# A hybrid encoder layer on one core: the attention mask added by VectorE, one copy of the attention's products out of PSUM, paced weight splits, and queries loaded a head ahead

## The chip, the core and the metric

The kernel runs on one core of one Trainium2 chip. The metric is the device time of one execution in microseconds, taken as the median of several runs. The engines are named as the profile names them: PE is TensorE (its weight loads are PEld), DVE is VectorE, ACT is ScalarE, POOL is GpSimd, and SP is SyncE, whose queue issues nearly all DMAs.

## What is computed

One layer of a post-norm encoder on 1024 prompt frames and 32 frames of a running stream (1056 together), width 1024, 8 heads of 64, in float32:

```python
p = x @ w_in      # GLU pair | q | k | v | forget logits | two branch gates
u = a * sigmoid(b); y_conv = (silu(LN(depthwise_conv31(u) + b_dw))) @ w_conv_out
c = cumsum(log_sigmoid(p_f + b_f))                     # per head
s = (q @ k.T) / 8 + c_q - c_k
s = where(k_pos <= q_pos, s, -1e30)                    # causal mask
o = softmax(s) @ v
m = sigmoid(g_conv) * y_conv + sigmoid(g_attn) * (o @ w_attn_out)
x1 = LN1(alpha * x + m @ w_o)
y = LN2(alpha * x1 + square(relu(x1 @ w_up)) @ w_down)
```

The streams attend to 512 cached keys and values besides their own 32. Keys, values, log forget values and the last 30 convolution rows are outputs too.

## The kernel before, in words

Everything is held transposed, features on partitions. A float32 operand is split into two fp32r parts, `hi` (ACT, a rounding copy) and `lo` (DVE or POOL, the rest), and a product is three matmuls: hi by hi, hi by lo, lo by hi. `Weights` (`W`) loads the tiles of the big matrices by halves into `raw` (four halves held), splits them (`split`, lines 336 to 350) and holds up to `RB` = 4 split tiles; `W.engine` says which engine makes `lo` (POOL in the attention stage). `W.ahead` is called at every `I.service()`; `W.take` splits on demand what is not split yet.

The order of instructions on PE, ACT, DVE and POOL is that of the program; DMAs on SP's queue are ordered by the framework. A planner (`Issue`, `I`) keeps an estimated clock for each engine while the program is written. `I.fill(*need)` puts steps of other work, the *filler*, into PE's order as long as the needed tiles are not due by these clocks and a quota is left. In the attention stage the filler is the branch gates' product (`gates`, tiles 6 to 15, six matmuls of 352 columns a step) and then the first two tiles of the convolution branch's projection (`early`, `ps_yc`).

The attention stage (lines 842 to 1173) works through units: eight prompt heads of eight row blocks (`Rows`, block `r` has 128 queries and `n` = 128 (r + 1) keys), and behind heads 2 to 5 one `Stream` each, two heads of the running stream against the cache. Row blocks are pipelined: one turn of the loop at line 1152 issues the scores of block `a0`, then the reciprocal of `a1`, the product with the values of `a3` (every second block, two blocks at a time, 256 queries), the transposes of `a2`, the exponential of `a0`, the normalization of `a1` and the `lo` subtractions of `a2`.

- `scores` (line 1025): two matmuls for each 512 keys into `ps_s`, of which two buffers exist, then the mask as a product of a bf16 identity and a bf16 mask tile with 1e30 above the diagonal, added into the last 128 columns (the scores are negated). `softmax_a` takes the row minimum on DVE.
- `weigh` is the exponential on ACT with its sum, `norm` the division by it on DVE, `turn` the transposes through `ps_tr` and the split into `th` (ACT) and `tl` (DVE).
- `fold` (line 994): the product with the values, `ps_pv`, has the part with `v`'s hi on partitions 0 to 63 and that with its lo on 64 to 127. ACT copies both halves out into two tiles `oa` and `ob`, POOL adds them and splits the sum into `oh` and `ol`. `ps_pv` takes its buffer from the two of `ps_tr`.
- `load_head` (line 863) issues a head's nine loads: keys `k1` and `k2`, queries `q1` and `q2`, values `v`. `load(n + 1)` calls it at the third row block of the unit before, or, behind a `Stream`, when that starts.

Of the kernel before, what the change touches and what calls it, by code (L numbers as in the profile page):

```python
# [9 lines left out]
F32 = mybir.dt.float32  # L10
F32R = mybir.dt.float32r
# [6 lines left out]
P = 128  # L18
D = 1024
SEQ = 1024  # L20
# [9 lines left out]
H = 8  # L30
# [15 lines left out]
RB = 4  # L46
# [221 lines left out]
def hybrid_layer(ctx: ExitStack, tc, io):  # L268
# [54 lines left out]
    class Weights:  # L323
        def __init__(self):
            self.raw, self.parts, self.taken, self.done, self.halves = [], [], 0, 0, 0
            self.engine, self.limit = "dve", NWO + 1

        def load(self, queue=None):
            i = len(self.raw)
# [22 lines left out]
        def ahead(self):  # L352
            while len(self.raw) < 2 * self.limit and held["raw"] < RAWB:
                self.load()
            while self.halves < len(self.raw) and I.ready(self.raw[self.halves]) <= I.t["pe"] and \
                    (self.halves % 2 or self.halves // 2 in kept or held["parts"] < RB):
                self.split()
                if len(self.raw) < 2 * self.limit:
                    self.load()

        def take(self):
            self.ahead()
# [479 lines left out]
    with pool("b") as pb, pool("pb", space=PSUM) as psb:  # L842
# [17 lines left out]

        def load_head(h, i):
            hr = slice(h * DH, (h + 1) * DH)
            k1 = pb.tile([P, 2 * NKS], F32R, tag=f"k1{i % 2}", bufs=1, name=f"k1_{h}")
            q1 = pb.tile([P, SEQ], F32R, tag=f"q1{h % 2}", bufs=1, name=f"q1_{h}")
            k2, q2 = k2s[i % 2], q2s[h % 2]
            v = pb.tile([P, 10, P], F32R, tag=f"v{i % 2}", bufs=1, name=f"v_{h}")
            queue = nc.gpsimd if h == 0 else None
            dma(k1[0:DH, 0:SEQ], qk_s["kh"][hr, 0:SEQ], queue)  # L870
            dma(k1[DH:P, 0:SEQ], qk_s["kh"][hr, 0:SEQ], queue)
            dma(q1[0:DH], qk_s["qh"][hr, 0:SEQ], queue)
            dma(q1[DH:P], qk_s["ql"][hr, 0:SEQ], queue)
            dma(k2[0:DH, 0:SEQ], qk_s["kl"][hr, 0:SEQ], queue)
            dma(k2[DH:DH + 2, 0:SEQ].rearrange("s (t i) -> s t i", i=P), crows[0][h, :, 0:NT, :], queue)
            dma(q2[0:DH], qk_s["qh"][hr, 0:SEQ], queue)
            dma(q2[DH + 2:DH + 4, :].rearrange("s (t i) -> s t i", i=P), crows[1][h, :, 0:NT, :], queue)
            dma(v[:, 0:NT, :], v_s[h])
            return k1, k2, q1, q2, v

# [113 lines left out]
        def fold(pv, n, tag, outs, parts=1, into=None):  # L994

            at = 0 if into is None else into[0]
            pr = slice(at, at + DH)
            a, b = (pb.tile([P, 256], F32, tag=x, bufs=1, name=f"{x}_{tag}")[pr, :parts * n] for x in ("oa", "ob"))
            act(a, pv[0:DH, :parts * n], AF.Copy)
            act(b, pv[DH:P, :parts * n], AF.Copy)  # L1000
            tt(a, a, b, ADD, "pool")
            if parts > 1:
                tt(a[:, :n], a[:, :n], a[:, n:], ADD, "pool")
                a = a[:, :n]
            if into is None:
                oh, ol = (pb.tile([DH, 256], F32R, tag=x, bufs=2, name=f"{x}_{tag}")[:, :n] for x in ("oh", "ol"))
            else:
                oh, ol = (t[pr, into[1]] for t in last_o)
            I.run("pool", n * 3.0 + 120, [oh], [a])
            nc.gpsimd.tensor_copy(oh, a)  # L1010
            tt(ol, a, f32(oh), SUB, "pool")
            for cols, dst in outs:
                for i, t in enumerate((oh, ol)):
                    if dst[0].start < 6 * DH:
                        dma(o_s[i][dst], t[:, cols])
                    else:
                        dma(last_o[i][dst[0].start - 6 * DH:dst[0].stop - 6 * DH, dst[1]], t[:, cols])

        class Rows:
# [5 lines left out]
            def scores(self):  # L1025
# [5 lines left out]
                for a in range(0, n, 512):  # L1031
                    w = min(512, n - a)
                    mm(ps[:, a:a + w], q1[:, qc], k1[:, a:a + w], True, False)
                    mm(ps[:, a:a + w], q2[:, qc], k2[:, a:a + w], False, a + w < n)
                mm(ps[:, n - P:n], ident_b, mask_b, False, True)
                self.sm = softmax_a(ps[:, :n], n, tag)

            def weigh(self):
# [42 lines left out]
        class Stream:  # L1081


            def __init__(self, ops, g):
                self.ops, self.g = ops, g

            def scores(self):
                k1, k2, q1, q2, _ = self.ops
# [46 lines left out]
        def work():  # L1135
            for n, (kind, h) in enumerate(units):
# [5 lines left out]
                for i, r in enumerate(ROWS):  # L1142
                    if i % 2 == 0:
                        pair = []
                    if i == 2:
                        load(n + 1)
                    yield Rows(ops, h, r, pair)

        act(tiny, eps, AF.Exp)
        a1 = a2 = a3 = None  # L1150
        I.quota = Q0
        for a0 in chain(work(), (None,) * 3):
            I.quota += ((16 - GA + YM / 2) * 12 - Q0) / (H * NT + H // 2)
            if a0:
# [6 lines left out]
                a2.turn()  # L1161
            if a0:
                a0.weigh()
            if a1:
                a1.norm()
            if a2:
# [2 lines left out]
            I.service()  # L1169
            a1, a2, a3 = a0, a1, a2  # L1170
        act(tiny, eps, AF.Sigmoid)
        while I.step(True):
            pass

# [805 lines left out]
```

## Time and profile before

| | |
|---|---|
| median of 3 runs | 1444.24 us (1443.33 to 1444.28) |
| profiled execution | 1444.01 us, its span 1441.4 us |
| PE busy | 1425.4 us, 99% of the span |
| DVE, ACT, POOL busy | 1119.5, 683.0, 124.2 us |
| granted clock of PE | 0.998 of full speed (2.4 GHz) |
| attention stage | some 329 to 575 us of the span |

The span runs from the first to the last instruction of the profiled execution; its time has some 2.6 us more around it. An engine's busy time is the union of its instructions. Matmuls are pipelined, so one matmul's listed duration is longer than the distance to the next one's start.

### The profile page before, as it was taken

To read this page: it belongs to the slowest core of one execution; us is meant where nothing else is said; L and a number is where in the kernel's file an instruction comes from. 1 tells how busy PE (TensorE), PEld (TensorE's weight loads), DVE (VectorE), ACT (ScalarE), POOL (GpSimd) and SP (SyncE) were. 2 spreads that over 40 slices of the span, in tenths; PEclk is the share of its full clock that TensorE was granted. 3 is DMA by queue.
4 is the path that set the end of the run, shared out by engine and by line. 5 is a ranking of instruction groups with operands and counts; after the bars stand their busy time and mean duration, and the time that the engine had idled before them with its cause. 6 is when DMAs were issued, how large, how long until landed. Compare 5 with 4: busy or idle time off the path is not lost.

```text
span 1441.4 us, 27988 instructions
## 1 busy us (share of the span) xinstructions
PE 1425.4 (99%) x10623; PEld 1404.0 (97%) x10623; DVE 1119.5 (78%) x1929; ACT 683.0 (47%) x1446; POOL 124.2 (9%) x183
## 2 busy tenths in 40 slices
PE   9999999999999999999999999999999999999996
PEld 8999999999999999999999999999999999999996
DVE  6998899865666655855797888888976789889668
ACT  5123433465665656543345666676657323321134
POOL 0000000023455533000000000000000000000000
PEclk9999999999999999999999999999999999999999
DMA  7125554287455557425343348766689999884212
GB/s 249 46 61 161 171 172 157 88 273 209 111 152 157 154 153 264 144 83 177 94 135 124 130 151 296 251 239 231 225 287 344 335 317 333 276 321 176 67 45 77
DMA packets 157441, 267.91 MB, mean 186 GB/s; under 512 B 22680, under 2 KB 81272, under 8 KB 157308
## 3 DMA queue, kind: packets, MB, share of 16 engines
q1 hardware_dynamic: 156348, 263.98, 55.4%
q0 software_dynamic: 544, 1.59, 0.5%
q8 instruction: 84, 1.38, 0.4%
q10 hardware_dynamic: 416, 0.56, 0.1%
q14 instruction: 49, 0.40, 0.1%
HBM read 168.29 MB, written 97.74 MB: 185 GB/s over the span
## 4 chain that ended last, share of the span: by engine, by line
PE 97%; DVE 1%; DMA 1%; ACT 0%; issue 0%; SPq 0%; DVEq 0%
PE ps_u L206 18%; PE ps_d L206 17%; PE ps_g L206 13%; PE ps_dn L206 6%; PE ps_o L206 6%; PE ps_up L206 5%; PE ps_v L206 3%; PE ps_yc L206 3%; PE ps_k L206 3%; PE ps_glua L206 3%; PE ps_q L206 3%; PE ps_glub L206 3%; PE ps_yo L206 3%; PE ps_s L206 3%; PE ps_pv L206 2%; PE ps_tr L210 2%
## 5 line engine op out<-in xcount | busy, mean ns | idle before, releaser
L235 DVE SCALAR_TENSOR_TENSOR ca<-u,prm,ca 128x1086 f32<-128x1086 f32 x120 | 161.7, 1347 | 2.4
L206 PE MATMUL ps_g<-xh,whi 128*128 128x352 f32 x384 | 131.7, 343 | 0.0
L218 ACT ACTIVATE swhi<-s 128x512 fp32r<-128x512 f32 x100 | 61.9, 624 | 146.9 <-DVE s L227 134.0
L206 PE MATMUL ps_g<-xh,wlo 128*128 128x352 f32 x384 | 123.7, 322 | 0.0
L206 PE MATMUL ps_g<-xl,whi 128*128 128x352 f32 x384 | 121.5, 322 | 0.0
L206 PE MATMUL ps_u<-tl,swhi 128*128 128x264 f32 x416 | 118.4, 285 | 0.0
L206 PE MATMUL ps_u<-th,swhi 128*128 128x264 f32 x416 | 118.2, 284 | 0.0
L206 PE MATMUL ps_u<-th,swlo 128*128 128x264 f32 x416 | 118.2, 284 | 0.0
L218 ACT ACTIVATE whi<-raw 128x512 fp32r<-128x512 f32 (+1 forms) x120 | 69.6, 624 | 69.6 <-PE ps_glua L206 29.7
L227 DVE TENSOR_TENSOR tl<-ps_tr,th 128x512 fp32r<-128x512 f32 (+2 forms) x96 | 51.4, 552 | 60.2 <-ACT th L218 59.5
L206 PE MATMUL ps_d<-hu_h,swhi 128*128 128x264 f32 x480 | 93.0, 285 | 0.1
L206 PE MATMUL ps_d<-hu_l,swhi 128*128 128x264 f32 x480 | 92.9, 285 | 0.0
L218 ACT ACTIVATE r<-r 128x528 f32<-128x528 f32 (+1 forms) x120 | 73.9, 616 | 37.8 <-DVE r L227 35.5
L227 DVE TENSOR_TENSOR wlo<-raw,whi 128x512 fp32r<-128x512 f32 (+1 forms) x100 | 64.8, 686 | 29.1 <-ACT whi L218 28.9
L227 DVE TENSOR_TENSOR r<-r,ps_u 128x528 f32<-128x528 f32 x91 | 62.6, 699 | 29.6 <-PE ps_u L206 29.6
L206 PEld LDWEIGHTS ps_u<-th,swhi 128*128 128x128 f32 x416 | 78.3, 188 | 0.0
L206 PEld LDWEIGHTS ps_u<-th,swlo 128*128 128x128 f32 x416 | 78.3, 188 | 0.0
L206 PEld LDWEIGHTS ps_u<-tl,swhi 128*128 128x128 f32 x416 | 78.2, 188 | 0.0
L227 POOL TENSOR_TENSOR acc<-acc,lnrest 128x288 f32<-128x288 f32 x4 | 3.0, 787 | 857.6 <-ACT lnrest L218 857.6
L206 PEld LDWEIGHTS ps_d<-hu_h,swhi 128*128 128x128 f32 x480 | 74.6, 189 | 0.3 <-issue 0.2
L206 PEld LDWEIGHTS ps_d<-hu_l,swhi 128*128 128x128 f32 x480 | 74.6, 189 | 0.0
L206 PEld LDWEIGHTS ps_g<-xh,whi 128*128 128x128 f32 x384 | 72.7, 189 | 0.7
(434 smaller groups left out, 4997.8 us busy)
## 6 DMA issues: line engine op xcount, KB each, us to landing
h_s<-sp SPq DMA_DIRECT2D x84, 528.0 KB
raw<-in_w_in_dram SPq DMA_DIRECT2D x63, 256.0 KB
hu_h<-h_s SPq DMA_DIRECT2D x30, 528.0 KB
hu_l<-h_s SPq DMA_DIRECT2D x30, 528.0 KB
sraw<-in_w_up_dram SPq DMA_DIRECT2D x52, 256.0 KB
hu<-h_s SPq DMA_DIRECT2D x24, 528.0 KB
sraw<-in_w_ds_dram SPq DMA_DIRECT2D x48, 256.0 KB
g_s<-gt SPq DMA_DIRECT2D x48, 176.0 KB
```

What stands on the lines that cost most here:

```text
L206: self.nc.tensor.matmul(ps, lhsT=w, rhs=x, start=start, stop=stop)
L210: self.nc.tensor.transpose(ps, x, ident)
L218: self.nc.scalar.activation(out, in_, func, **kw)
L227: (self.nc.vector if eng == "dve" else self.nc.gpsimd).tensor_tensor(out, a, b, op)
L235: self.nc.vector.scalar_tensor_tensor(out, a, s, b, op0, op1)
```

## The change

The mask product of a row block becomes an addition by DVE on the last 128 columns of `ps_s` (the streams keep theirs). `fold` copies all 128 partitions of `ps_pv` to `ob` in one ACT instruction; POOL copies the half that lies on the other partitions to `oa`, and adds. In the attention stage (`paced`) `W.ahead` no longer splits; one half is split behind the exponential of a row block of more than 256 columns, and on demand. The four query loads leave `load_head` and are issued at the third row block of the head before, ahead of the next unit's loads.

```diff
--- before.py
+++ after.py
@@ -323,7 +323,7 @@
     class Weights:
         def __init__(self):
             self.raw, self.parts, self.taken, self.done, self.halves = [], [], 0, 0, 0
-            self.engine, self.limit = "dve", NWO + 1
+            self.engine, self.limit, self.paced = "dve", NWO + 1, False
 
         def load(self, queue=None):
             i = len(self.raw)
@@ -352,11 +352,18 @@
         def ahead(self):
             while len(self.raw) < 2 * self.limit and held["raw"] < RAWB:
                 self.load()
-            while self.halves < len(self.raw) and I.ready(self.raw[self.halves]) <= I.t["pe"] and \
-                    (self.halves % 2 or self.halves // 2 in kept or held["parts"] < RB):
+            while not self.paced and self.step():
+                pass
+        def step(self):
+            i = self.halves
+            if i < len(self.raw) and I.ready(self.raw[i]) <= I.t["pe"] and (i % 2 or i // 2 in kept or held["parts"] < RB):
                 self.split()
                 if len(self.raw) < 2 * self.limit:
                     self.load()
+                return True
+            return False
 
         def take(self):
             self.ahead()
@@ -860,21 +867,31 @@
 
 
 
+        queries = {}
+        def load_queries(h, queue=None):
+            hr = slice(h * DH, (h + 1) * DH)
+            q1 = pb.tile([P, SEQ], F32R, tag=f"q1{h % 2}", bufs=1, name=f"q1_{h}")
+            q2 = q2s[h % 2]
+            dma(q1[0:DH], qk_s["qh"][hr, 0:SEQ], queue)
+            dma(q1[DH:P], qk_s["ql"][hr, 0:SEQ], queue)
+            dma(q2[0:DH], qk_s["qh"][hr, 0:SEQ], queue)
+            dma(q2[DH + 2:DH + 4, :].rearrange("s (t i) -> s t i", i=P), crows[1][h, :, 0:NT, :], queue)
+            queries[h] = q1, q2
         def load_head(h, i):
             hr = slice(h * DH, (h + 1) * DH)
             k1 = pb.tile([P, 2 * NKS], F32R, tag=f"k1{i % 2}", bufs=1, name=f"k1_{h}")
-            q1 = pb.tile([P, SEQ], F32R, tag=f"q1{h % 2}", bufs=1, name=f"q1_{h}")
-            k2, q2 = k2s[i % 2], q2s[h % 2]
+            k2 = k2s[i % 2]
             v = pb.tile([P, 10, P], F32R, tag=f"v{i % 2}", bufs=1, name=f"v_{h}")
             queue = nc.gpsimd if h == 0 else None
             dma(k1[0:DH, 0:SEQ], qk_s["kh"][hr, 0:SEQ], queue)
             dma(k1[DH:P, 0:SEQ], qk_s["kh"][hr, 0:SEQ], queue)
-            dma(q1[0:DH], qk_s["qh"][hr, 0:SEQ], queue)
-            dma(q1[DH:P], qk_s["ql"][hr, 0:SEQ], queue)
+            if h == 0:
+                load_queries(h, queue)
+            q1, q2 = queries[h]
             dma(k2[0:DH, 0:SEQ], qk_s["kl"][hr, 0:SEQ], queue)
             dma(k2[DH:DH + 2, 0:SEQ].rearrange("s (t i) -> s t i", i=P), crows[0][h, :, 0:NT, :], queue)
-            dma(q2[0:DH], qk_s["qh"][hr, 0:SEQ], queue)
-            dma(q2[DH + 2:DH + 4, :].rearrange("s (t i) -> s t i", i=P), crows[1][h, :, 0:NT, :], queue)
             dma(v[:, 0:NT, :], v_s[h])
             return k1, k2, q1, q2, v
 
@@ -995,10 +1012,12 @@
 
             at = 0 if into is None else into[0]
             pr = slice(at, at + DH)
-            a, b = (pb.tile([P, 256], F32, tag=x, bufs=1, name=f"{x}_{tag}")[pr, :parts * n] for x in ("oa", "ob"))
-            act(a, pv[0:DH, :parts * n], AF.Copy)
-            act(b, pv[DH:P, :parts * n], AF.Copy)
-            tt(a, a, b, ADD, "pool")
+            a, b = (pb.tile([P, 256], F32, tag=x, bufs=1, name=f"{x}_{tag}")[:, :parts * n] for x in ("oa", "ob"))
+            act(b, pv[:, :parts * n], AF.Copy)
+            a = a[pr]
+            I.run("pool", parts * n * 1.0 + 120, [a], [b])
+            nc.gpsimd.tensor_copy(a, b[DH - at:P - at])
+            tt(a, a, b[pr], ADD, "pool")
             if parts > 1:
                 tt(a[:, :n], a[:, :n], a[:, n:], ADD, "pool")
                 a = a[:, :n]
@@ -1031,8 +1050,8 @@
                 for a in range(0, n, 512):
                     w = min(512, n - a)
                     mm(ps[:, a:a + w], q1[:, qc], k1[:, a:a + w], True, False)
-                    mm(ps[:, a:a + w], q2[:, qc], k2[:, a:a + w], False, a + w < n)
-                mm(ps[:, n - P:n], ident_b, mask_b, False, True)
+                    mm(ps[:, a:a + w], q2[:, qc], k2[:, a:a + w], False, True)
+                tt(ps[:, n - P:n], ps[:, n - P:n], mask_b, ADD)
                 self.sm = softmax_a(ps[:, :n], n, tag)
 
             def weigh(self):
@@ -1082,7 +1101,7 @@
 
 
             def __init__(self, ops, g):
-                self.ops, self.g = ops, g
+                self.ops, self.g, self.n = ops, g, NKS
 
             def scores(self):
                 k1, k2, q1, q2, _ = self.ops
@@ -1143,12 +1162,15 @@
                     if i % 2 == 0:
                         pair = []
                     if i == 2:
+                        if h + 1 < H:
+                            load_queries(h + 1)
                         load(n + 1)
                     yield Rows(ops, h, r, pair)
 
         act(tiny, eps, AF.Exp)
         a1 = a2 = a3 = None
         I.quota = Q0
+        W.paced = True
         for a0 in chain(work(), (None,) * 3):
             I.quota += ((16 - GA + YM / 2) * 12 - Q0) / (H * NT + H // 2)
             if a0:
@@ -1161,6 +1183,9 @@
                 a2.turn()
             if a0:
                 a0.weigh()
+                if a0.n > 2 * P:
+                    W.step()
             if a1:
                 a1.norm()
             if a2:
@@ -1169,6 +1194,7 @@
             I.service()
             a1, a2, a3 = a0, a1, a2
         act(tiny, eps, AF.Sigmoid)
+        W.paced = False
         while I.step(True):
             pass
 
```

## Rows read from the trace of the kernel before

**Rows 1.** The page: the span, the busy time of each engine with its share and its instructions, and the shares of the chain that ended last by engine.

```profile
span 1441.4 us, 27988 instructions
PE 1425.4 (99%) x10623; PEld 1404.0 (97%) x10623; DVE 1119.5 (78%) x1929; ACT 683.0 (47%) x1446; POOL 124.2 (9%) x183
...
PE 97%; DVE 1%; DMA 1%; ACT 0%; issue 0%; SPq 0%; DVEq 0%
```

**Rows 2.** Busy time of the engines from 329 to 575 us: length of the window, then for PE, PEld, DVE, ACT and POOL the busy us and the number of instructions, PE's granted clock, the DMA share and GB/s.

```profile
329.00:575.00 246.00, 245.00 (x1717) 231.27 (x1716) 149.74 (x318) 152.69 (x377) 108.45 (x148) 1.00 0.59 170
```

**Rows 3.** All waits of PE in that window: who waited for whom, us in total, times, the longest.

```profile
PE ps_s L206 <- ACT p L218: 0.6, 1, 0.6
PE ps_tr L210 <- DVE tl L227: 0.4, 1, 0.4
```

**Rows 4.** The instructions on the mask's tile `bfs`, and the weight loads of the scores: duration in ns (least, median, most), first and last start in us, shapes.

```profile
L206 PE MATMUL ps_s<-bfs x64: 229/230/233, 330.0 to 556.8; 128*128 128x128 bf16 x64
L222 DVE CAST bfs<-ident x1: 219/219/219, 155.8 to 155.8; 128x128 bf16<-128x128 f32 x1
...
L206 PEld LDWEIGHTS ps_s<-k,q x192: 186/188/247, 329.7 to 556.4; 128*128 128x128 f32 x192
```

**Rows 5.** PE in order of time (start us, length us of the merged rows, names, count): the first and the last of the 40 masks ahead of gate or `ps_yc` products, one with the scores ahead of it, the first and the last of the 23 ahead of transposes, one of these with what follows, and four transposes behind a value product.

```profile
330.39 0.23 PE L206 MATMUL ps_s<-bfs 128*128 128x128 bf16 x1
330.43 0.41 PE L206 MATMUL ps_g<-xh,whi 128*128 128x352 f32 x1
330.68 0.32 PE L206 MATMUL ps_g<-xl,whi 128*128 128x352 f32 x1
330.84 0.32 PE L206 MATMUL ps_g<-xh,wlo 128*128 128x352 f32 x1
...
551.41 0.23 PE L206 MATMUL ps_s<-bfs 128*128 128x128 bf16 x1
...
551.71 0.33 PE L206 MATMUL ps_yc<-ysl,whi 128*128 128x352 f32 x1
...
385.02 0.40 PE L206 MATMUL ps_s<-k,q 128*128 128x512 f32 x1
385.26 0.23 PE L206 MATMUL ps_s<-bfs 128*128 128x128 bf16 x1
...
333.76 0.23 PE L206 MATMUL ps_s<-bfs 128*128 128x128 bf16 x1
...
556.84 0.23 PE L206 MATMUL ps_s<-bfs 128*128 128x128 bf16 x1
...
389.91 0.23 PE L206 MATMUL ps_s<-bfs 128*128 128x128 bf16 x1
389.98 0.63 PE L210 MATMUL ps_tr<-ident,p 128*128 128x128 f32 x4
390.36 0.41 PE L206 MATMUL ps_g<-xh,whi 128*128 128x352 f32 x1
...
394.20 0.62 PE L210 MATMUL ps_tr<-ident,p 128*128 128x128 f32 x4
394.58 0.41 PE L206 MATMUL ps_g<-xh,whi 128*128 128x352 f32 x1
```

**Rows 6.** Groups of instructions by shape from 325 to 575 us on DVE, ACT and POOL: count, busy us, mean ns of one, idle us before them and what ended it.

```profile
L227 DVE TENSOR_TENSOR tl<-ps_tr,th 128x256 fp32r<-128x256 f32 x16 | 6.6, 413 | 1.2 <-ACT th L218 1.2
L227 DVE TENSOR_TENSOR tl<-ps_tr,th 128x128 fp32r<-128x128 f32 x16 | 4.6, 287 | 19.0 <-ACT th L218 18.9
...
L218 ACT ACTIVATE ob<-ps_pv 64x256 f32<-64x256 f32 x32 | 12.2, 381 | 0.8
L218 ACT ACTIVATE oa<-ps_pv 64x256 f32<-64x256 f32 x32 | 12.1, 377 | 45.5 <-PE ps_pv L206 45.5
L218 ACT ACTIVATE whi<-raw 128x512 fp32r<-128x512 f32 x20 | 11.5, 630 | 0.0
L218 ACT ACTIVATE th<-ps_tr 128x256 fp32r<-128x256 f32 x16 | 6.1, 384 | 1.6 <-PE ps_tr L210 1.5
...
L227 POOL TENSOR_TENSOR wlo<-raw,whi 128x512 fp32r<-128x512 f32 x20 | 26.6, 1348 | 27.9 <-ACT whi L218 27.9
L227 POOL TENSOR_TENSOR oa<-oa,ob 64x256 f32<-64x256 f32 x32 | 23.3, 728 | 103.5 <-ACT ob L218 100.1 <-DMA o_s<-ol 3.3
L1010 POOL CAST oh<-oa 64x256 fp32r<-64x256 f32 x24 | 9.4, 390 | 1.5
L1010 POOL CAST oh_s<-oa_s 64x64 fp32r<-64x64 f32 x4 | 0.9, 230 | 0.3
```

**Rows 7.** The normalizations of the streams (DVE): duration in ns (least, median, most), first and last start in us.

```profile
L231 DVE TENSOR_SCALAR p_s<-p_s,rs_s x4: 503/504/1540, 410.1 to 506.2; 128x544 f32<-128x544 f32 x4
```

**Rows 8.** One turn of the loop in order of time (start us, length us): DVE's normalization, ACT's row, and PE at the scores of head 2's seventh row block.

```profile
388.61 0.48 DVE L231 TENSOR_SCALAR p<-p,rs 128x512 f32<-128x512 f32 x1
...
389.11 0.38 ACT L218 ACTIVATE oa<-ps_pv 64x256 f32<-64x256 f32 x1
389.52 0.38 ACT L218 ACTIVATE ob<-ps_pv 64x256 f32<-64x256 f32 x1
389.92 0.49 ACT L218 ACTIVATE th<-ps_tr 128x384 fp32r<-128x384 f32 x1
390.31 0.79 ACT L218 ACTIVATE p<-ps_s,mn 128x640 f32<-128x640 f32 x1
390.99 0.20 ACT L218 ACTIVATION_READ_ACCUMULATOR p<-ps_s,mn 128x1 f32 x1
...
391.41 0.39 PE L206 MATMUL ps_s<-k,q 128*128 128x512 f32 x1
```

**Rows 9.** The end of the stage: POOL's subtractions into `yol` (duration in ns, first and last start), and PE's first `ps_yo` product.

```profile
L227 POOL TENSOR_TENSOR yol<-oa,yoh x8: 723/734/923, 525.4 to 571.6; 64x256 fp32r<-64x256 f32 x8
...
576.56 0.28 PE L206 MATMUL ps_yo<-yoh,whi 128*128 128x264 f32 x1
```

**Rows 10.** SP's queue in order of time (start us, us of issue): two query loads, and the keys' loads of the same stretch.

```profile
380.29 0.59 SPq L201 DMA_DIRECT2D q<-ql_s  x1
...
381.56 0.86 SPq L201 DMA_DIRECT2D q<-qh_s  x1
...
400.69 1.99 SPq L201 DMA_DIRECT2D k<-kh_s  x2
```

## The prediction

> **What bounds the kernel now.** I read the page first: TensorE (PE) is busy 99% of the span, VectorE (DVE) 78%, ScalarE (ACT) 47%, GpSimd (POOL) 9%, and the chain that ended last is PE for 97% [rows 1]. The thing to see is that the sum of PE's work nearly is the time, so an edit counts by what it takes from PE's queue or by the waits it puts into it. The change lies in the attention stage, 329 to 575 us. One window over it [rows 2]: PE busy 245.0 of 246.0 us at full granted clock, DVE 149.7, ACT 152.7, POOL 108.5. The waits of PE in that window are two, 0.6 us for ACT's exponential and 0.4 us for DVE's `tl` [rows 3]. So there is about 1 us of waiting to win in the stage, and the rest of any gain must be PE work that goes away. A busy PE can hide pieces too short to be called a wait, so the third reading was PE's own start times around the mask product [rows 4, 5].
>
> **The mask leaves PE.** There are 64 products of `bfs` into `ps_s`, one a row block [rows 4]; the streams' four stay. The mean of one is listed as 230 ns, but matmuls overlap, so I cost them by starts. Ahead of a gate product: the mask starts at 330.39, the gate's first product at 330.43, its second at 330.68, its third at 330.84. From the mask to the second is 0.29 us, and a gate product elsewhere follows the one before at 0.16: the mask and the late start behind it cost 0.13. The last of this kind, ahead of a `ps_yc` product at 551.41, reads 0.30, again 0.13 to 0.14 over [rows 5]. The matmul behind it has to load 128x128 of 4-byte weights (188 ns each, [rows 4]), and behind a mask that takes 0.04 us from start to start that load has no cover. I count 40 such places and one ahead of other scores, at 0.125: 41 x 0.125 = 5.1 us. The other 23 (first 333.76, last 556.84) stand ahead of transposes. There, four transposes from the mask's start to the next gate product take 0.45 us (389.91 to 390.36), and four behind a value product 0.38 (394.20 to 394.58): 0.07 each, 1.6 us [rows 5]. Sum 6.7 us off PE. Bounds: from below the starts of the masks alone, 40 x 0.04 + 24 x 0.07 = 3.3 us, if the load behind them would have stood uncovered anyway; from above 64 x 0.126 = 8.1. I take 6.7, since the last scores product ahead of a mask mostly takes longer than the mask does (0.24 us from 385.02 to 385.26), and so gives the next load its cover.
>
> The Trainium skill, "TensorE: Matmul & The Clock Gate", section Back-to-back issue gap, gives N/2.4 + 2.5 ns between isolated matmuls, 56 ns at 128 columns. By it the sum would be 64 x 0.056 = 3.6 us, and the time 1440.4. The starts above say more than that rule for one place in a stream, so it is carried as the first rival only.
>
> **The mask comes to DVE.** 64 additions of 128x128, PSUM and a bf16 tile into PSUM. No row has that form; the nearest is `tl<-ps_tr,th` 128x128, 287 ns; bounds are the CAST into `bfs` at 219 and the same subtraction on 256 columns at 413 [rows 4, 6]. 64 x 0.287 = 18.4 us (14.0 to 26.4): DVE goes from 149.7 to 168 of some 240 us, still under PE. In its queue the addition stands ahead of this row's minimum, the row before's reciprocal and normalization, and the `tl` subtractions. What PE needs of those is the normalized `p` for the transposes a whole row later. In the row shown, the normalization of 512 columns ends at 389.09 and PE takes its transposes at 389.98, 0.9 us later [rows 5, 8]. So 0.29, or 0.58 where two masks stand in the chain, is covered. If the cover were gone in every row it would be 18.4 us.
>
> **One copy of the products.** Each of 32 folds has two ACT copies, 377 and 381 ns. One copy of 128x256 takes what `th` 128x256 takes, 384 ns, as the partitions cost nothing: 0.37 us off ACT a fold, 32 x 0.37 = 12 us, and a little for the streams' four [rows 6]. POOL gains a copy of 64x256; nearest is its CAST of that size, 390 ns (bounds: 230 for 64x64 and the 728 of an addition): 36 x 0.39 = 14 us at most on 108.5 of 246 [rows 2, 6]. On PE this is nothing directly, but it shortens the tightest chain I found. ACT's row: `oa` 389.11, `ob` 389.52, `th` 389.92, exponential 390.31, its accumulator read ending 391.19; PE starts the scores that need this PSUM slot at 391.41 [rows 8]. Only 0.2 us of margin, kept up by six gate products put in between. Both copies are in this chain, so it shrinks by about 0.4. At the end of the stage the last fold must reach `yo`: its last `yol` starts at 571.6 and PE takes the first `ps_yo` at 576.56, so the longer POOL chain (+0.39 less 0.37) is hidden by `ps_yc` products [rows 9].
>
> A rule against this edit: the Trainium skill, "SBUF — State Buffer", section Who interferes with whom, has DVE's two-port instructions and POOL locking each other out for a whole instruction. The trace does show normalizations of 544 columns at 503 ns median and 1540 at most [rows 7]. By the rule all 36 new POOL copies could hold DVE up by 0.39, 14 us on DVE; behind 0.9 us of margin none of it would reach PE, and the sum stays.
>
> **Weight splits paced.** 20 splits in the stage, ACT 630 ns and POOL 1348 ns each [rows 6], are now made at most one behind each row of over 256 columns (six of a head's eight rows, and the streams): 48 + 4 = 52 chances for some 24 halves. They remove nothing, they only stand behind the exponential. Cost nothing, as up to four tiles are held ahead and one gate tile is 72 products, 72 x 0.16 = 11.5 us of PE. If the cover went, a tile would cost 0.63 + 2 x 1.35 = 3.3 us.
>
> **Queries ahead.** Four loads a head move in front of the next unit's loads. On SP's queue they pass the cached head's loads, 0.59 and 0.86 for two of them, some 2.5 us of issue for four; what is behind is needed many us later. And the trace shows queries issued at 380.29 while the keys go at 400.69 [rows 10]: the queue order already runs ahead of the program's. So this edit does little on the chip; it only lets the planner believe in earlier scores behind a cached head and place fewer gate products there. I cost it at nothing, bounds -1 to +2 us (one wait of some 0.5 us at each of four such places).
>
> **Sum.** The profiled execution took 1444.01 us around its span of 1441.4; the median of the runs is 1444.24. 1444.0 - 6.7 = 1437.3. The two waits (1.0 us) may go with the shorter ACT chain, and about as much may arise since PE comes earlier; I leave them even.
>
> **Rivals.** (1) Only the masks' own starts are saved, 3.3 us: 1440.7. For it, many short loads already run uncovered; against it, the 0.16 spacing that returns two products behind each mask. (2) DVE's lateness reaches PE: if the fifth and seventh rows of a head, where slots are tight, each lose 0.29, 16 x 0.29 = 4.6 and the time is 1441.9. For it, 0.2 us of margin in the row shown; against it, that chain loses 0.4 on ACT, and the exponential there waited for ACT's queue, not for the minimum. If more than 33 of 64 rows lose it (33 x 0.29 = 9.6) it is slower than before by over 0.2%. (3) The other side: weights late. A gate tile whose halves were not split is split on demand, and PE waits 3.3 us. From three late tiles on (9.9 us against 6.7 + 2.9) the kernel is slower; with all 12, 1437.3 + 40 = 1477. Against it: 52 chances for 24 halves. (4) More than forecast: all 64 at 0.126 and both waits gone, 9.1 us: 1434.9.
>
> **Chances.** Forecast (1436 to 1439.5) 0.58; more (4) 0.12; only the starts (1) 0.14; DVE's lateness short of slower 0.10, slower 0.03; late weights 0.03. A measurement of this kernel can tell about 0.2%, 2.9 us, from no change, so below 1441.3 is faster and above 1447.1 slower. Faster: 0.58 + 0.12 + most of (1), 0.80; same: the rest of (1) and (2), 0.14; slower 0.06. The range reaches up to (2), 1442, and down just past (4), 1434.5: it leaves out some 0.15.
>
> **What the profile after would show.** PE without `ps_s<-bfs`, a span some 6.7 shorter, all of it inside the attention stage; gate products behind scores starting 0.16 apart at once; 64 DVE additions of about 287 ns; one `ob` copy of about 384 ns; PE's waits in the stage still near 1 us. I am wrong if PE's waits there add up to more than 3 us (for `p`, `tl`, `wlo`, or `k`), if the product behind the scores still starts late, or if a later stage gives the time back.

## The result and the profile after

The change made the kernel slower: 1448.78 us (1447.08 to 1450.81) against 1444.12, a ratio of 1.003 with a 95% interval of 1.0019 to 1.0041. I had forecast 1437.3 in a range of 1434.5 to 1442.0, and given slower a chance of 0.06. The profiled execution took 1447.08 us around a span of 1445.3.

The page of the kernel after; compare [rows 1].

```profile
span 1445.3 us, 27915 instructions
PE 1424.0 (99%) x10559; PEld 1402.4 (97%) x10559; DVE 1148.3 (79%) x1993; ACT 668.0 (46%) x1410; POOL 136.6 (9%) x219
```

PE has 64 instructions fewer and is 1.4 us less busy, yet the span is 3.9 us longer. The window of [rows 2], with the same columns:

```profile
329.00:575.00 246.00, 238.26 (x1612) 224.46 (x1612) 175.60 (x380) 136.19 (x339) 119.38 (x181) 1.00 0.59 167
```

And the waits of PE in the stage, which were the two of [rows 3]:

```profile
PE ps_tr L210 <- DVE p L231: 2.1, 4, 0.9
PE ps_ss L206 <- POOL k L227: 1.9, 4, 0.9
PE ps_tr L210 <- DVE tl L227: 1.6, 2, 1.0
PE ps_ss L206 <- issue: 0.6, 1, 0.6
PE ps_pv L206 <- DVE tl L227: 0.5, 1, 0.5
PE ps_s L206 <- DMA k<-c_s: 0.4, 1, 0.4
```

PE is idle 7.7 us of this window, where it was idle 1.0. I had written that over 3 us of waits there would mean that I was wrong. The first `ps_yo` product comes at 581.37 instead of 576.56 [rows 9], so all of the loss is made in the attention stage: from there to the end the profiled execution takes 863.9 us, where that of the kernel before took 864.9.

The parts that I had costed, mask addition and copy, came out as costed:

```profile
L227 DVE TENSOR_TENSOR ps_s<-ps_s,bfs 128x128 f32<-128x128 f32 x64 | 18.5, 288 | 20.0 <-PE ps_s L206 19.8
...
L218 ACT ACTIVATE ob<-ps_pv 128x256 f32<-128x256 f32 x32 | 12.3, 384 | 53.6 <-PE ps_pv L206 53.5
```

What had changed beside them is the normalization, which I had costed at nothing. DVE's groups by shape in the stage (busy us, then the mean in ns), first those of the kernel before:

```profile
L231 DVE TENSOR_SCALAR p<-p,rs 128x1024 f32<-128x1024 f32 x8 | 6.4, 801 | 0.3
L231 DVE TENSOR_SCALAR p<-p,rs 128x640 f32<-128x640 f32 x8 | 4.5, 564 | 0.3
L231 DVE TENSOR_SCALAR p<-p,rs 128x512 f32<-128x512 f32 x8 | 5.2, 653 | 0.3
```

The same groups of the kernel after:

```profile
L231 DVE TENSOR_SCALAR p<-p,rs 128x1024 f32<-128x1024 f32 x8 | 8.1, 1007 | 0.3
L231 DVE TENSOR_SCALAR p<-p,rs 128x640 f32<-128x640 f32 x8 | 7.6, 953 | 0.3
L231 DVE TENSOR_SCALAR p<-p,rs 128x512 f32<-128x512 f32 x8 | 7.4, 924 | 0.3
```

And one of them in order of time, in the kernel after (start us, length us; a bracket gives the idle time ahead of it and what ended it):

```profile
552.81 2.52 POOL L227 TENSOR_TENSOR wlo<-raw,whi 128x512 fp32r<-128x512 f32 x2
...
553.75 1.86 DVE L231 TENSOR_SCALAR p<-p,rs 128x512 f32<-128x512 f32 x1
553.87 0.95 PE L206 MATMUL ps_s<-k,q 128*128 128x512 f32 x4
...
555.76 0.63 PE L210 MATMUL ps_tr<-ident,p 128*128 128x128 f32 x4 [0.94 <-DVE p L231]
```

A normalization of the same shape took 0.48 us in [rows 8]. Here it ends at 555.61, 0.28 us behind the second of two weight subtractions that POOL makes back to back (to 555.33), and PE waits 0.94 us for it. Those two subtractions are halves of a weight tile that the change moved behind the exponentials.

The waits of this profile are not the whole of the 4.7 us. Three of the eight executions of the kernel after have a mean granted clock of 0.997 and took 1447.08, 1447.19 and 1448.04 us; four with 0.996 took 1448.72 to 1449.04, and one with 0.995 took 1450.81. The profiled one is the fastest of them. So some 1.6 us of the median (1448.8 less 1447.2, an estimate) go with a lower granted clock, which this profile doesn't show. The trace of u_queries_back below, the kernel after with the queries as before, does (0.996, 1448.28 us; the columns are those of [rows 2]):

```profile
470.00:480.00 10.00, 7.64 (x56) 7.24 (x55) 5.40 (x8) 2.75 (x7) 5.77 (x7) 1.00 0.66 175
480.00:484.00 4.00, 4.00 (x21) 4.00 (x20) 2.69 (x7) 1.66 (x5) 0.00 (x0) 0.57 0.24 62
```

PE had stood idle 2.4 us of the first window, 2.0 of it in one wait for keys; then its granted clock was 0.57 on average over 4 us, so for most of them it was 1.2 GHz and not 2.4. Of the kernel before, all executions recorded with their clock but one had 0.997 or 0.998.

### The profile page after: what moved, and what is told of

Read it like the earlier page. It is cut to its first block, busy times and chain, and to the rows that moved or that the text cites. A ratio compares the mean times of both kernels' runs of the same rounds, so it can differ in the third digit from the quotient of the medians.

```text
span 1445.3 us, 27915 instructions
## 1 busy us (share of the span) xinstructions
PE 1424.0 (99%) x10559; PEld 1402.4 (97%) x10559; DVE 1148.3 (79%) x1993; ACT 668.0 (46%) x1410; POOL 136.6 (9%) x219
## 4 chain that ended last, share of the span: by engine, by line
PE 92%; DVE 3%; DMA 2%; POOL 1%; issue 1%; ACT 1%; SPq 0%; DVEq 0%; ACTq 0%; POOLq 0%
PE ps_u L206 18%; PE ps_d L206 17%; PE ps_g L206 10%; PE ps_o L206 6%; PE ps_dn L206 6%; PE ps_up L206 5%; PE ps_v L206 3%; PE ps_k L206 3%; PE ps_glua L206 3%; PE ps_q L206 3%; PE ps_glub L206 3%; PE ps_yo L206 3%; PE ps_yc L206 3%; PE ps_pv L206 2%; PE ps_tr L210 2%; PE ps_s L206 2%
## 5 line engine op out<-in xcount | busy, mean ns | idle before, releaser
L235 DVE SCALAR_TENSOR_TENSOR ca<-u,prm,ca 128x1086 f32<-128x1086 f32 x120 | 161.8, 1348 | 2.4
L206 PE MATMUL ps_g<-xh,whi 128*128 128x352 f32 x384 | 128.8, 336 | 0.0
```

The source lines that it names most:

```text
L206: self.nc.tensor.matmul(ps, lhsT=w, rhs=x, start=start, stop=stop)
L235: self.nc.vector.scalar_tensor_tensor(out, a, s, b, op0, op1)
```

## The experiments

Three numbers from each trace stand beside the time. **Stage**: from PE's first `ps_s` start to its first `ps_yo` start. **Waits**: what the distances between PE's starts in the stage have over the median of the same pair in the kernel before, where that is over 0.15 us; where a pair isn't found there, as the mask's product is gone, the choice of the median moves the sum by about 1 us. **Stretch**: the durations of the 68 normalizations over the shortest of their shape, summed. A to D are the parts of the change's diff: A is the mask on DVE, B the one copy, C the paced splits, D the early queries. "Old order" means that the planner is charged as in the kernel before, so that the filler products stand exactly where they stood (their order on PE is identical). Times were taken beside the kernel before, which had a median of 1443.8 to 1444.2 in each set.

| run | what | time | ratio, 95% | stage | waits | stretch |
|---|---|---|---|---|---|---|
| before | | 1444.1 | | 246.7 | 1.5 | 6.6 |
| after | A+B+C+D | 1448.8 | 1.0019 to 1.0041 | 251.6 | 11.0 | 14.7 |
| e1_mask_out | mask left out, old order | 1439.3 | 0.9957 to 0.9980 | 242.3 | 2.6 | |
| e2_mask_dve_old_order | A, old order | 1441.2 | 0.9974 to 0.9992 | 244.8 | 4.5 | 7.5 |
| e3_mask_alone | A | 1445.0 | 1.0001 to 1.0018 | 248.5 | 8.7 | 8.7 |
| u_mask_back | B+C+D | 1444.8 | 0.9999 to 1.0016 | 248.8 | 3.8 | 12.2 |
| s_copy_alone | B | 1441.5 | 0.9973 to 0.9990 | 246.0 | 1.9 | 7.2 |
| s_pace_alone | C | 1449.6 | 1.0025 to 1.0052 | 252.0 | 6.4 | 16.8 |
| s_queries_alone | D | 1448.0 | 1.0016 to 1.0039 | 250.1 | 4.9 | 9.6 |
| u_pace_back | A+B+D | 1443.9 | 0.9994 to 1.0011 | 247.4 | 7.8 | 10.6 |
| x_pace_low_dve | C, low parts on DVE | 1490.7 | 1.0310 to 1.0338 | 293.4 | 40.1 | 3.1 |
| y_mask_copy_old_order | A+B, old order | 1436.6 | 0.9937 to 0.9962 | 241.0 | 2.2 | 8.5 |
| x_queries_old_order | D, old order | 1444.3 | 0.9994 to 1.0012 | 246.6 | 1.5 | 6.8 |
| u_queries_back | A+B+C | 1447.3 | 1.0011 to 1.0029 | 251.0 | 10.0 | 18.6 |
| x_pace_low_later | C, low parts on DVE, later | 1461.4 | 1.0103 to 1.0134 | 262.9 | 17.1 | 5.6 |
| z_copy_old_order | B, old order | 1441.4 | 0.9972 to 0.9989 | 245.0 | 0.8 | 9.0 |
| u_pace_queries_back | A+B | 1442.9 | 0.9984 to 1.0002 | 246.6 | 7.1 | 10.3 |
| y_with_pace | A+B old order, C | 1444.3 | 0.9993 to 1.0010 | 248.1 | 9.3 | 14.5 |
| x_pace_low_zero | C, low parts zeroed | 1444.8 | 0.9995 to 1.0013 | 247.3 | 1.9 | 9.7 |
| x_before_low_zero | before, low parts zeroed | 1443.6 | 0.9988 to 1.0006 | 246.7 | 1.4 | 5.3 |

A time has a span and some time around it, and that isn't the same everywhere: 2.6 us in the kernel before, 1.8 in the kernel after and in every run with B but z_copy_old_order (2.1), 2.4 in s_pace_alone, 1.9 in x_pace_low_zero. No run shows what sets it. By medians of the spans the kernel after is 5.5 us longer than before (1447.0 against 1441.5) and not 4.7, and B's gains are some 0.5 to 0.8 us smaller than the times say.

Seven times lay outside every range that I had written for them: e2_mask_dve_old_order, s_copy_alone, s_pace_alone, u_pace_back, y_mask_copy_old_order, y_with_pace and, closely, x_pace_low_zero.

### The mask: its price, DVE's part and the planner's

The mask left out, with its charge kept:

```diff
-                    mm(ps[:, a:a + w], q2[:, qc], k2[:, a:a + w], False, a + w < n)
-                mm(ps[:, n - P:n], ident_b, mask_b, False, True)
+                    mm(ps[:, a:a + w], q2[:, qc], k2[:, a:a + w], False, True)
+                I.run("pe", 107, [ps[:, n - P:n]], [ident_b, mask_b])
```

> The kernel before with the mask left out altogether (part of the computation is missing), while the planner is still charged for a mask product on PE, so that the order on every engine stays that of before. It measures the price of the 64 products on PE by itself. If 6.7 us was sized right: 1437.4 (a gain of 6 to 7.5). If only the masks' own starts count: 1440.8 (gain 3.3). If the time does not follow PE's work: 1444.

The second run adds the line `nc.vector.tensor_tensor(ps[:, n - P:n], ps[:, n - P:n], mask_b, ADD)`.

> The kernel before with the mask added by DVE, but the planner charged as if it still were a product on PE: the order of before with one instruction moved. Theory A (the order that the planner writes anew is at fault, not the addition): DVE's addition lies in the margins, 1437 to 1440, and PE's waits in the attention stage stay under 3 us. Theory B (the addition's latency itself reaches PE): 1444 to 1450, waits of PE on p and tl near the 9 us more that the changed kernel shows.

The third has the mask's part of the change as it is, so the planner reckons with DVE's addition.

> Only the mask's edit, with the planner charged for the addition on DVE (209 ns) and for no product on PE. Theory A: the planner's new order places the gate products otherwise and the waits come back, 1441 to 1448, clearly above the run with the old order. Theory B: the same time as with the old order, 1444 to 1450. If the three other edits are what costs (theory C: POOL's longer work and the shorter cover behind cached heads): 1437 to 1440 here too.

Left out, the mask is worth 4.7 us, not 6.7. DVE's addition costs 1.9 of them. The planner's new order costs 3.8 more, and turns the gain into a loss. The filler products show how: in e3_mask_alone up to 48 of them stand ahead of an attention product ahead of which they didn't stand before, and PE waits later, where they are missing. Its waits in the stage:

```profile
PE ps_tr L210 <- DVE tl L227: 2.6, 2, 1.4
PE ps_pv L206 <- DVE tl L227: 1.5, 2, 1.0
PE ps_str L210 <- ACT ob L218: 1.4, 3, 0.5
PE ps_tr L210 <- ACT ob L218: 0.9, 2, 0.5
```

For the planner each mask took 107 ns off PE's clock, 6.8 us in all, and an addition takes 209 on DVE's clock (the rows say 288). With PE's clock earlier, operands look late more often, and the filler is spent sooner. Which of the two charges does it wasn't tried apart.

> The changed kernel with the mask as a product on PE again: the copy, the paced splits and the earlier queries alone. Theory C: these cost 3 to 5 us, 1447 to 1450 and with the mask's 6.7 us on top up to 1455. Theories A and B: about the time of before, 1443 to 1446.

Undone in the kernel after, the mask gives 4.0 us back: there too it is a loss.

### Each of the other parts alone

> The kernel before with the one copy out of PSUM alone. Theory C1 (POOL's longer fold delays PE): 1446 or more. Theory A (only new orders cost, and this edit shifts the planner's ACT clock by 0.38 us a fold): 1443 to 1445, waits of PE in the stage under 4 us.

> The kernel before with the paced splits alone. If the splits' place on POOL, ahead of the cached keys' lo parts, makes the streams' scores wait by itself: 1446 to 1448 with waits on POOL's k. If that needs the other edits too: 1443.5 to 1445.

> The kernel before with the queries' loads one head ahead alone. If the planner takes gate products away behind the streams and PE then waits for keys: 1446 or more, PE waiting on DMA. If it is without effect: 1443.5 to 1444.7.

> The changed kernel with the splits unpaced again (mask, copy and queries remain). Theory P (the paced splits stand on POOL ahead of the streams' keys, which costs the 3.5 us of waits at the streams' scores in the changed kernel's trace): these waits go, 1444.5 to 1446. Rival (the order of PE alone is at fault, whatever stands on POOL): 1448 to 1450 again.

The copy alone gains 2.7 us (1.8 by the spans, of which the stage shows 0.7); I had it at nothing. The paced splits alone lose 5.5, and taken out of the kernel after they give 4.9 back (3.5 between the executions with a clock of 0.997 or more): they are the one part that accounts for a loss of the size seen both ways. I had expected PE to wait for POOL's `k` in s_pace_alone. It didn't; all its waits in the stage are for DVE and ACT:

```profile
PE ps_pv L206 <- DVE tl L227: 2.3, 6, 0.7
PE ps_tr L210 <- DVE p L231: 1.6, 2, 0.8
PE ps_tr L210 <- ACT th L218: 0.3, 1, 0.3
PE ps_tr L210 <- DVE tl L227: 0.2, 1, 0.2
```

The queries alone lose 3.8, of which two waits for keys show 1.4:

```profile
PE ps_s L206 <- DMA k<-kh_s: 0.7, 1, 0.7
PE ps_s L206 <- DMA k<-c_s: 0.7, 1, 0.7
```

The prices don't add up (0.9 - 2.7 + 5.5 + 3.8 = 7.5, measured 4.7), since each part also moves the filler. So the next runs hold the order.

### The queries and the copy with the old order

In the first, the four query DMAs are issued early as in the change, but without the planner, which is charged in `load_head`, where they stood:

```diff
-            dma(q1[0:DH], qk_s["qh"][hr, 0:SEQ], queue)
...
+            def charge(out, in_):
+                I.run("dma", max(450, I.size(out) * out.shape[0] * 4 / 360), [out], [in_])
```

(Excerpt; `charge` stands in `load_head` for each of the four loads.)

> The queries alone, loaded a head ahead, but charged to the planner's DMA clock where the kernel before charged them, so that the filler products stand where they stood before; the DMAs themselves are issued early. Alone with its own charges the step took 1448.0 us. Theory 'order': the 3.8 us are the planner's, whose filler products stand elsewhere; then 1443.5 to 1445 here. Rival 'queue': the four transfers stand ahead of the cached head's keys in SP's queue and make these late; then 1446.5 or more.

It has the time of the kernel before, and the same two waits as [rows 3]. So the early loads cost nothing clear of the noise by themselves, as I had said, and the 3.8 us were the planner's: up to 24 filler products fewer stand ahead of an attention product at one place and up to 30 more at another. In the kernel with A, B and C the queries cost 1.5 us (1447.3 to 1448.8), with A and B 1.0 (1442.9 to 1443.9); in both cases the intervals of the two ratios overlap.

> The kernel after with the queries' early load alone undone (mask by VectorE, one copy and paced splits stay). If the steps' prices add up, it gains the 3.8 us that the queries alone cost: 1444 to 1446. If the queries' price was that of one particular order of the filler products, it isn't found again here: 1448 or more, or any other value, with the waits of TensorE elsewhere.

The copy, with two copies charged to ACT and none to POOL (excerpt, the new lines):

```diff
+            I.run("act", parts * n * 0.81 + 62, [a], [pv[0:DH, :parts * n]])
+            I.run("act", parts * n * 0.81 + 62, [b], [pv[DH:P, :parts * n]])
+            nc.scalar.activation(b, pv[:, :parts * n], AF.Copy)
+            a = a[pr]
+            nc.gpsimd.tensor_copy(a, b[DH - at:P - at])
```

> The one copy out of PSUM alone, with the planner still charged for the two copies, so that the filler products stand as before. With its own charges the copy alone took 1441.5 us (2.7 us less than before). Theory 'real': ScalarE's 13 us less are worth what they were worth, 1441 to 1442.5. Rival 'order': the gain came from another place of the filler products; 1443.5 to 1444.5 here.

The copy's gain is real, 2.8 us, with every filler product where it was. The stage is 1.7 us of it, and part of that is PE's waits, from 1.5 to 0.8.

> The mask by VectorE and the one copy out of PSUM, with neither the paced splits nor the early queries, and with the planner's charges of the kernel before (the mask still charged to TensorE, two copies to ScalarE), so that the filler products stand where they stood before. Alone the mask with the old order gave 1441.2 us, and the copy alone 1441.5 us. Theory 'two real gains': the mask's 2.9 us and a part of the copy's 2.7 us add up, 1438 to 1440.5. Rival 'the copy's gain was the order it came with': with the old order the copy is worth nothing, 1441 to 1442.

Together with the mask it gives 7.3 us, more than the sum of both (2.9 + 2.8), though by no more than the intervals of the three ratios allow. The stage is 5.7 us shorter and PE's waits are 2.2 us, where A alone had 4.5. That the shorter ACT chain takes up DVE's lateness fits this and wasn't tried apart. **This kernel beats both**, by 0.5% and 0.8%. PE's waits in its stage:

```profile
PE ps_tr L210 <- DVE p L231: 0.6, 2, 0.3
PE ps_tr L210 <- DVE tl L227: 0.6, 1, 0.6
PE ps_s L206 <- ACT p L218: 0.2, 1, 0.2
```

> The kernel after with the paced splits and the early queries both undone: the mask by VectorE and the one copy, each with the planner's charges that it brings. With the old order these two took 1436.6 us. If the new order costs with both what it cost with the mask alone (3.8 us), 1439.5 to 1441.5; if the copy takes that cost away, since ScalarE's copies come earlier, 1436 to 1438; and if the steps' prices alone add up (0.9 slower, 2.7 faster), 1441.5 to 1443.

The same two edits with their own charges take 1442.9: the planner's order costs 6.3 us. The prices alone added up here (0.9 slower, 2.7 faster), and the expectation that the copy would cover the order's cost fell.

### Why the paced splits cost: hold or place

Two theories were left: POOL's subtractions hold DVE's normalizations, or ACT's high copies stand in the way where they are now.

In the first test DVE subtracts at the place of the split, with POOL charged:

```diff
-            tt(lo, raw, f32(hi), SUB, self.engine)
+            if self.paced:
+                I.run("pool", n * 1.97 + 150, [lo], [raw, f32(hi)])
+                nc.vector.tensor_tensor(lo, raw, f32(hi), SUB)
+            else:
+                tt(lo, raw, f32(hi), SUB, self.engine)
```

> The paced splits alone (measured before at 1449.6 us), with the planner's charges kept, so that every instruction stands where it stood, but the low part of each split in the attention is subtracted by VectorE and not by GpSimd. Theory 'lock': what costs the 5.5 us is that GpSimd's 1.3 us subtractions now fall on VectorE's normalizations and hold them; then their stretch over the shortest of their shape falls from 16.8 us to 8 or less and the time to 1444 to 1446.5, although VectorE gets some 10 us of work more. Rival 'place': what costs is where the high copy stands on ScalarE, behind an exponential and ahead of the next row's; then the stretch falls as well, but the time stays at 1448.5 or more.

Neither theory had this: 1490.7 us. By its letter it is "place" (a small stretch, and no gain), but the wait behind it is a new one. The stretch fell to 3.1 as "hold" said, but the subtraction now stands in DVE's queue ahead of the normalization, and waits for a high copy that stands behind ACT's exponential. The group of those subtractions:

```profile
L351 DVE TENSOR_TENSOR wlo<-raw,whi 128x512 fp32r<-128x512 f32 x18 | 14.3, 793 | 53.3 <-ACT whi L218 53.3
```

One of them in order of time, with ACT's copy ahead of it and DVE's normalization behind:

```profile
443.15 0.62 ACT L218 ACTIVATE whi<-raw 128x512 fp32r<-128x512 f32 x1
443.80 0.69 DVE L351 TENSOR_TENSOR wlo<-raw,whi 128x512 fp32r<-128x512 f32 x1 [1.51 <-ACT whi L218]
444.41 0.55 DVE L231 TENSOR_SCALAR p<-p,rs 128x640 f32<-128x640 f32 x1
```

DVE stood 53 us for `whi`, and PE waited 24.6 us for `p`. PE's granted clock fell as well, to 0.94 on average from 329 to 575 us, where s_pace_alone has 1.00, so the time holds more than the waits. I then moved DVE's subtraction to the end of the turn, behind the `tl` subtractions (excerpt; the freeing of `raw` and the next load move with it):

```diff
                 for r in a2.rest:
                     tt(*r, SUB)
+            W.low()
             I.service()
```

> The paced splits alone (1449.6 us) with the planner's charges and ScalarE's high copies where they stood, but the low parts of the attention's paced splits subtracted by VectorE at the end of the row's turn, behind the subtractions of the transposes' low parts, where ScalarE's high copy has been made. Theory 'hold': GpSimd's subtraction on VectorE's normalizations is what costs; the stretch of these falls from 16.8 to 8 us or less, TensorE's waits in the attention fall from 6.4 to 2 to 4 us, and the time is 1444 to 1447. Rival 'place': the high copy between two rows' exponentials is what costs, and the time stays at 1448.5 or more with a small stretch.

It still stood 11.6 us for `whi`, and PE waited 6.2 us for `tl` and 5.1 for `p`. The stretch was 5.6, so these two runs show that the hold goes with POOL's subtraction, but put a larger wait in its place: they don't tell what the hold cost.

The deciding pair keeps POOL's instruction where it was, and only sets the low parts to zero, in the paced kernel and, as the control, in the kernel before (excerpt; elsewhere the line is as it was):

```diff
+            if self.engine == "pool":
+                I.run("pool", n * 1.97 + 150, [lo], [raw, f32(hi)])
+                nc.gpsimd.memset(lo.bitcast(F32), 0.0)
```

> The paced splits alone (1449.6 us), where GpSimd sets the low parts of the attention stage's weight splits to zero in place of subtracting them: the low parts are left out of the result, and GpSimd's instruction becomes one without a source. All else, the planner's charges too, stays. Theory 'hold': the normalizations' stretch falls from 16.8 us to that of the kernel before or less (at most 6.6), and the time to that of the control x_before_low_zero within 1 us. Rival 'place of the high copy': stretch falls, but the time stays 3 us or more above the control.

> The kernel before, where GpSimd sets the low parts of the attention stage's weight splits to zero in place of subtracting them (the low parts are left out of the result); the planner's charges stay. The control: the stretch of the normalizations there is 6.6 us, and only 1.5 us of TensorE's time in the stage are waits, so 1442.5 to 1444.2 is expected by every theory.

With the same order of filler as s_pace_alone the time falls from 1449.6 to 1444.8, PE's waits from 6.4 to 1.9. The control moves 0.3 us. So 4.8 of the 5.5 us are POOL's subtraction, and 1.3 (a little over the 1 that I had allowed) are left for the high copies, the filler's order and the memsets; by spans 4.2 of 5.7, and 1.9 left. What PE still waits for in the stage:

```profile
PE ps_pv L206 <- DVE tl L227: 0.7, 2, 0.3
PE ps_tr L210 <- DVE tl L227: 0.5, 2, 0.4
```

The stretch fell only to 9.7, not to 6.6: a memset of 0.54 us holds a normalization too. Two groups of normalizations in s_pace_alone:

```profile
L231 DVE TENSOR_SCALAR p<-p,rs 128x384 f32<-128x384 f32 x8 | 10.0, 1251 | 0.3
L231 DVE TENSOR_SCALAR p<-p,rs 128x512 f32<-128x512 f32 x8 | 8.3, 1037 | 0.3
```

The same in x_pace_low_zero:

```profile
L231 DVE TENSOR_SCALAR p<-p,rs 128x384 f32<-128x384 f32 x8 | 8.0, 1000 | 0.3
L231 DVE TENSOR_SCALAR p<-p,rs 128x512 f32<-128x512 f32 x8 | 4.2, 524 | 0.3
```

And POOL's memsets there:

```profile
L351 POOL MEMSET wlo<- 128x512 f32 x18 | 9.4, 539 | 0.1
```

In s_pace_alone some 13 of the 16.8 us of stretch lie in normalizations beside which POOL made a `wlo`; in the kernel after 10.1 of 14.7. Those beside which POOL ran nothing have under 0.3 us of it together, in every one of these traces. That the zeroing was not tried in the kernel after itself leaves its own share open: there the hold is read from its trace, and PE's waits for POOL's `k` stand beside it.

> The mask by VectorE and the one copy with the old charges (1436.6 us), and the paced splits on top. Theory 'hold by GpSimd': the low parts fall on VectorE's normalizations here too, whose stretch grows from 8.5 to 13 us or more, and 3 to 6 us are lost: 1439.5 to 1442.5. Rival: the one copy has freed ScalarE enough, or this order is another one, and the paced splits cost nothing: 1436 to 1437.5.

On the best kernel the paced splits cost 7.7 us (1436.6 to 1444.3), more than on any other base. "Hold" was right in kind, and its 3 to 6 us too small; the stretch grew from 8.5 to 14.5. Why it is more here isn't shown: the mask on DVE leaves less room for a late normalization, but the kernel with A, B and D has it there too and loses 4.9, and the filler's order changes with the splits.

## Why the prediction was wrong, step by step

**What bounds the kernel** held: PE's order and PE's waits in the stage make the time, and the difference of the profiles lies there. The prediction reckoned with the full granted clock throughout; some 1.6 us of the median go with its fall.

**The mask leaves PE, 6.7 us: too large.** It measured 4.7 (interval 2.9 to 6.2). Summed by instruction, PE's starts in the stage lose 4.1 us at the masks and 2.7 at the gate and `ps_yc` products behind them, 6.8, about what I had. But the scores, now the last thing ahead of these, take 1.75 more to the next start and the transposes 0.65; 1.1 of those 2.4 are waits. The assumption that the last scores product "mostly takes longer than the mask does", and so "gives the next load its cover", was too strong. The Trainium skill's rule for isolated matmuls, in "TensorE: Matmul & The Clock Gate", section Back-to-back issue gap, was 3.6 us by the prediction's sum; it lies below the measured value and within its interval.

**The mask on DVE, hidden: off by 1.9 us.** The duration was right (288 ns against 287), the cover wasn't everywhere. That is rival (2) with less than half its price.

**One copy, nothing: it gains 2.8 us.** I had seen the tight ACT chain that both copies stand in, 0.2 us of margin [rows 8], and looked only at waits long enough to be listed.

**The paced splits, nothing: the first failed step.** Alone they lose 5.5 us, in the kernel after 4.9. "They remove nothing, they only stand behind the exponential" named no work that hides them. I had checked whether the weights would come late, rival (3), and they didn't. I hadn't asked what runs on DVE while POOL subtracts. The answer stood in the rows I had: 20 subtractions of 1348 ns, and a streams' normalization at 1540 where the median is 504 [rows 6, 7].

I had that rule in hand and applied it to the wrong instruction. The Trainium skill, "SBUF — State Buffer", section Who interferes with whom, has an exclusive lock between GpSimd and DVE's two-port instructions, `tensor_scalar` among those that can be. The traces agree: normalizations of 512 columns went from 653 to 1037 ns with the paced splits, the `tl` subtractions from PSUM stayed at 686. I weighed it for 36 new copies of 0.39 us and called their 14 us hidden; the moved subtractions, three times as long and in pairs, weren't asked about.

**Queries ahead, nothing: right for the DMAs, wrong for the planner.** x_queries_old_order took 1444.3. But I had written that the edit lets the planner "place fewer gate products there", and bounded that by +2; alone it was 3.8.

**The sum left out the order: the second failed step, and the larger.** Each of the four parts changes what the planner sees, and so where the some 760 filler products stand. With A and B that costs 6.3 us, nearly the whole gain. The prediction priced the instructions and held the filler in place. From the forecast to the measured time: A and B with the old order 0.7 better (1436.6 against 1437.3), their order 6.3 worse, D 1.0 (within the noise), C 4.9 (3.5 at a clock of 0.997 or more), together 11.5 us. That A and B come out so near the forecast is luck: the mask alone gives 2.9 of its 6.7 us, the copy alone, costed at nothing, 2.8, and both together 7.3. My steps from before to after, each with its own charges: A 0.9 slower, B 2.1 faster, D 1.0 slower, C 4.9 slower, together the 4.7.

One wait of the kernel after belongs to two parts: at 469.35 and 471.81 POOL makes a `wlo`, each behind an idle time that ACT's `whi` ends, and the streams' keys stand behind them in its queue; PE waits for these (`ps_ss` <- POOL `k`, 1.9 us). Without the paced splits 0.8 us of that wait remain.

## What to carry to other kernels

When work is moved on one engine, ask what the engines beside it run at the new place: a POOL instruction that was harmless in one stretch can hold DVE's `tensor_scalar` in another (1.86 us for one of 0.48), and what DVE has no slack for reaches PE. Where a planner writes the order, price an edit twice, once for its instructions with the order held and once for the order that its charges bring, and keep the old order when the charges are no truer than before. A subtraction moved off the contended engine into an in-order queue brings its wait along.

## What the runs showed of the hardware

POOL's instructions held a normalization even when they wrote only: in x_pace_low_zero one of 640 columns, at 425.45, took 1.34 us beside two memsets (425.46 to 426.44), where 0.55 is the shortest of that shape; those beside two memsets and an `ol_s` subtraction of 0.32 took up to 1.50, where 0.42 is the shortest. A normalization doesn't always get in between POOL instructions that follow back to back: in the kernel after, the one shown lasted through the rest of one and the whole of a second, and ended 0.28 us behind it. But in the kernel before one at 422.81 ended at 424.24, 0.29 us behind the first of two subtractions, with the second still to run to 425.38; what decides between the two isn't shown. And one that is listed 0.03 us ahead of POOL's `ol_s` (x_pace_low_zero, at 453.58) was held for 1.08 us as well, so the earlier listed start doesn't say who goes first.
